# Tying the later weight splits of two out-projection rows behind a hidden-block sum on VectorE

## The chip, the cores and the metric

The kernel runs on one core of a Trainium2 chip. The metric is the device time in microseconds of one execution. Three executions of the kernel before took 1464.35, 1462.27 and 1464.3 us, with a median of 1464.3 us. Five engines with their own instruction queues do the work: TensorE (PE, with its weight loads shown as PEld), VectorE (DVE), ScalarE (ACT), GpSimd (POOL) and SyncE (SP, which issues most of the transfers here). Each engine takes its instructions in the order in which the program lists them.

## The reference

The reference is one inference step of a two-layer streaming encoder. Layer 0 is a convolution module, layer 1 is an attention over a shared key and value projection, and each is followed by a SwiGLU feed-forward network (FFN). The model width is 1024, the hidden width of the FFN is 2816, and there are 640 frames (512 of one new stream and 8 x 16 of running streams), all in float32. The change lies in the FFN, which is called twice:

```python
def swiglu_ffn(h, g, w_in, w_out):
    a, b = jnp.split(rms_norm(h, g) @ w_in, 2, axis=-1)
    return h + (jax.nn.silu(a) * b) @ w_out
```

The outputs are the normed trunk of both groups, the convolution buffers, and the shared key and value rows.

## The kernel before, in words

**Products of three matmuls.** Each float32 factor is split in two parts: a rounded high part, which ScalarE writes (L369), and the rest as a low part, which VectorE makes by a subtraction (L370). This is the function `put`; for a piece of a weight it is called through `cut`. A product of two split factors takes three matmuls in L436: high weight by high data, low weight by high data, high weight by low data. One such matmul has 128 x 128 weights and 320 data columns.

**Blocks of the FFN.** The 640 columns are held as two halves of 320, and both matrices of a product are cut in 2 x 2 blocks. Seven block products take the place of eight, after Strassen. The operands of the seven are named X11, X21, XT2, XT1, XT3, XT4 and X22; the ones with T are sums of blocks. The hidden rows are worked on in three chunks of six tiles (`NCH` = 3, `CW` = 6), and a rest behind them. In a chunk, `seven` does the in-projection of a tile; the two tiles of a pair give the blocks of which `combined` makes the seven hidden operands. When the second block of a pair is ready, the branch `else` of `sink` makes the gate product (L474), the sum for XT2 (`minus`, L474), its parts (`own(XT2, t1)`), the sum for XT3 (L513) and that for XT4 (L474), each with its high part on ScalarE and its low part on VectorE. The trace calls these operands `hid` and the sums they are cut from `B`.

**The out-projection.** `out_chunk` multiplies the chunk's seven hidden operands with four weight rows, u = 0 to 3. The order of the products is written out in the string `QORD`; a token such as `61` means product 6 of row 1, where 5 is XT1, 1 is X11, 2 is X21, 6 is XT2, 3 is X22, 7 is XT3 and 4 is XT4. A mark ' stands for the first two of three hidden tile pairs, and " for the third one alone:

```python
QORD = ("50' a0 a1 10' 50\" 10\" 20 60' 30' 51' 60\" 30\" 51\" 70 "
        "11 21 40 61 31 52 71 12 22 41 62 32 53 72 13 23 42 63 33")
```

So 60", 30" and 51" are short (three, three and three matmuls) and 70 follows them. `a0` and `a1` are the end of the last in-projection tile, which gives the second block of the last pair. Every product is followed by an addition of its PSUM bank to the trunk `h` on VectorE (L573). Products 1, 6, 7 and 4 of a row accumulate in one bank, so that 60" can only go on once the addition after 10" has read it, and 70 once that after 60" has; 62 waits in the same way for the addition after 12.

**The weight row.** `w_seven(..., True)` loads a row of four pieces by SP (L412, tile `raw`, 768 KB), makes the sum `s` of two pieces by two transfers that GpSimd issues (L415, L416), and cuts the seven weight operands in the order XT1, X11, X21, XT2, X22, XT3, XT4. Three sums on VectorE stand between the cuts: L420 and L421 before the cut of XT2, L423 before that of X22. There are two `raw` buffers, so the transfer of row u = 3 waits until the pieces of row u = 1 have been read for the last time, and the transfer for the next in-projection tile (1024 KB) waits for row u = 2. The split operands go into eleven slots (`whi`/`wlo` and `shi`/`slo`), which are used in turn.

**What sets the order.** The instructions are not executed in the order in which the code is written. A planner simulates the program and places each instruction on its engine; work inside `tc.high_priority(offset=HP)` goes ahead of other work. `behind(ins)` (and `tc.issue_after`) adds an edge for the planner: an instruction inside it is placed behind `ins` if it runs on the same engine as `ins`. No semaphore is added by it, and instructions of other engines are not bound. `put_end[0]` holds the last low part that VectorE was given, and `lead` a list of ties that the next cuts take one by one.

Of the kernel before, what the change touches and what calls it, by code (L numbers as in the profile page):

```python
# [15 lines left out]
P = 128  # L16
# [45 lines left out]
X11, X21, XT2, XT1, XT3, XT4, X22 = range(7)  # L62
# [20 lines left out]
def tile_trunk(ctx, tc, xT, vecs, hist, w_pw1, w_pw2, w_in0, w_out0, w_os0, w_in1, w_out1, w_os1,  # L83
# [52 lines left out]
    @contextmanager  # L136
    def behind(*ins):
        with ExitStack() as st:
            for i in ins:
                st.enter_context(tc.issue_after(i))  # L140
            yield
# [189 lines left out]
    def ffn(l, w_in, w_out, w_os, tail, hf, lead=(), b0=None):  # L331
# [16 lines left out]
        mm = fpool("mm2", 6, space=PSUM)  # L348
        tp = fpool("tp1", 2)
        wx = fpool("wx", 2)  # L350
        lead, put_end = list(lead), [None, None]

        def ties():
            return lead.pop(0) if lead else ()
# [17 lines left out]
        def cut(w, o, src):  # L372
            c = slice(o, o + src.shape[-1])
            put(w[0][:, c], w[1][:, c], src)
# [30 lines left out]
                            cut(*ws[j // 512], raw[:, j:j + n])  # L405
            return ws[1], ws[0], ws[2], ws[3]

        def w_seven(src, out=False):
            n = src.shape[-1] // 4
            raw, ws = wraw(), {}  # L410
            s1 = wx.tile([P, 512], F32, tag="s1", name=nm("s1"))[:, :n]
            nc.sync.dma_start(raw[:, :4 * n], src)  # L412
            a12, a11, a21, a22 = (raw[:, n * i:n * i + n] for i in range(4))
            with tc.high_priority(offset=HP), behind(*ties()):
                nc.gpsimd.dma_start(s1, src[:, 2 * n:3 * n])  # L415
                nc.gpsimd.dma_start(s1, src[:, 3 * n:4 * n], accum_op=add)  # L416
                for x in ((XT1, X11, X21, XT2, X22, XT3, XT4) if out else
                          (X11, X21, XT2, XT1, XT3, XT4, X22)):
                    if x == XT2:
                        nc.vector.tensor_tensor(out=a21, in0=a11, in1=a21, op=add)  # L420
                        nc.vector.tensor_tensor(out=a11, in0=s1, in1=a11, op=add)  # L421
                    elif x == X22:
                        nc.vector.tensor_tensor(out=a12, in0=a12, in1=a11, op=add)  # L423
                    ws[x] = slot()
                    cut(*ws[x], {XT1: s1, X11: a11, X21: a12, XT2: a11, X22: a12, XT3: a21,
                                 XT4: a22}[x])
            return ws

        def product(pt, w, xs, first, ks=None):
# [53 lines left out]
        def combined(HH, HL, kp, second, held, neg, early=None):  # L483
            def own(c, src):
                for H_, j in ((HH, 2 * HIX[c]), (HL, 2 * HIX[c] + 1)):
                    if kp == 0:
                        t = two(j)
                        H_[c] = [t[:, 0, :], t[:, 1, :]]
                    elif kp == 2:
                        H_[c].append(one(j))  # L490
                put(HH[c][kp], HL[c][kp], src)

            def sink(half, a, b):
                if early is not None and half == 0:
                    t = early
                else:
                    tag = f"B{half}{int(second)}"
                    t = tp.tile([P, NH], F32, tag=tag, name=nm(tag), bufs=1)
                with tc.high_priority(offset=HP):
                    gate(t, a, b, neg)  # L500
                    if half == 0:
                        own((X11, X21)[second], t)
                        held[second] = t
                    elif not second:
                        nc.vector.tensor_tensor(out=held[0], in0=held[0], in1=t, op=sub)
                        own(XT1, held[0])
                        held[2] = t
                    else:
                        t1, b21, b12 = held
                        minus(t1, t1, t)  # L510
                        own(XT2, t1)
                        own(X22, t)
                        nc.vector.tensor_tensor(out=b12, in0=t, in1=b12, op=sub)  # L513
                        own(XT3, b12)
                        minus(b21, t1, b21)
                        own(XT4, b21)
            return sink
# [32 lines left out]
        def out_chunk(c, HH, HL, after):  # L550
            ws, pts = {}, {}
# [5 lines left out]
            def go(i, u, part):  # L557
                if u not in ws:
                    o = (4 * c + u) * 12 * P
                    ws[u] = w_seven(w_os[:, o:o + 12 * P], True)  # L560
                b, x, first, half, row = prod[i]
                if first and part != '"':
                    pts[b, u] = mmt()[:, :NH]
                pt = pts[b, u]
                with tc.issue_after(last[0]) if last else nullcontext():
                    ins = product(pt, ws[u][x], list(zip(HH[x], HL[x])), first,
                                  {"": None, "'": (0, 1), '"': (2,)}[part])
                last[:] = [ins.ins]
                if part == "'":
                    return  # L570
                hv = h[:, 2 * u + row, half * NH:half * NH + NH]
                with tc.high_priority(offset=HP):
                    nc.vector.tensor_tensor(out=hv, in0=hv, in1=pt, op=sub if row else add)  # L573
# [1083 lines left out]
```

## Time and profile before

| what | value |
|---|---|
| median of three executions | 1464.3 us |
| time of the profiled execution | 1464.42 us |
| span of the profiled execution | 1462.5 us |
| mean granted TensorE clock | 0.998 |
| TensorE matmul busy | 1435.3 us, 98% of the span |
| TensorE weight load busy | 1371.7 us, 94% |
| VectorE busy | 1141.8 us, 78% |
| ScalarE busy | 756.4 us, 52% |
| GpSimd busy | 294.4 us, 20% |

The span is what lies between the first and the last instruction in the trace; 1.9 us of the execution's own time lie around it. Rows of the timeline give the start in us, the duration in us, the engine, the line, the operation, the tiles written and read, and in brackets how long the engine was idle before it and what released it. Matmuls overlap, so the duration of one (0.31 us) is more than the distance from one to the next (0.147 us where TensorE waits for nothing).

### The profile page before, as it was taken

To read this page: it belongs to the slowest core of one execution; us is meant where nothing else is said; L and a number is where in the kernel's file an instruction comes from. 1 tells how busy PE (TensorE), PEld (TensorE's weight loads), DVE (VectorE), ACT (ScalarE), POOL (GpSimd) and SP (SyncE) were. 2 spreads that over 40 slices of the span, in tenths; PEclk is the share of its full clock that TensorE was granted. 3 is DMA by queue.
4 is the path that set the end of the run, shared out by engine and by line. 5 is a ranking of instruction groups with operands and counts; after the bars stand their busy time and mean duration, and the time that the engine had idled before them with its cause. 6 is when DMAs were issued, how large, how long until landed. Compare 5 with 4: busy or idle time off the path is not lost.

```text
span 1462.5 us, 28255 instructions
## 1 busy us (share of the span) xinstructions
PE 1435.3 (98%) x11040; PEld 1371.7 (94%) x11040; DVE 1141.8 (78%) x2524; ACT 756.4 (52%) x1627; POOL 294.4 (20%) x349
## 2 busy tenths in 40 slices
PE   9999999999999999999999999999999999999998
PEld 8998799999999999999987898878999999999998
DVE  6789767899788789766768668576899888888755
ACT  4666544554554464445655455443565554455443
POOL 5699102011111111013222111011001111111101
PEclk9999999999999999999999999999999999999999
DMA  7267425045444445424655554461235444444522
GB/s 243 82 176 186 121 73 159 9 128 153 127 105 131 131 116 143 116 87 171 203 163 199 175 199 163 134 206 41 69 81 142 132 116 132 133 120 114 151 65 72
DMA packets 66932, 192.56 MB, mean 132 GB/s; under 512 B 12144, under 2 KB 30320, under 8 KB 58480
## 3 DMA queue, kind: packets, MB, share of 16 engines
q1 hardware_dynamic: 52432, 160.58, 33.9%
q0 software_dynamic: 13504, 29.37, 9.9%
q8 instruction: 86, 1.41, 0.4%
q10 hardware_dynamic: 864, 0.83, 0.2%
q14 instruction: 46, 0.38, 0.1%
HBM read 179.14 MB, written 11.61 MB: 130 GB/s over the span
## 4 chain that ended last, share of the span: by engine, by line
PE 75%; DVE 11%; POOL 4%; DMA 4%; issue 3%; ACT 3%; SPq 0%; DVEq 0%; POOLq 0%; ACTq 0%
PE mm L436 45%; PE mm L199 7%; PE mm L201 7%; PE mm L200 7%; POOL ca L830 3%; DVE w L820 2%; PE am L1307 1%; DMA raw<-in_w_in 1%; PE w L1323 1%; PE am L1354 1%; DVE wlo L370 1%; PE am L1290 1%; DVE hid L591 1%; PE w L1266 1%; PE mm L874 1%
## 5 line engine op out<-in xcount | busy, mean ns | idle before, releaser
L436 PE MATMUL mm<-XH,whi 128*128 128x320 f32 x896 | 275.8, 310 | 1.7 <-DVE t L451 0.7
L436 PE MATMUL mm<-XH,wlo 128*128 128x320 f32 x896 | 276.7, 309 | 0.0
L436 PE MATMUL mm<-XL,whi 128*128 128x320 f32 x896 | 274.7, 309 | 0.0
L369 ACT ACTIVATE whi<-raw 128x512 fp32r<-128x512 f32 (+2 forms) x280 | 169.2, 614 | 142.6 <-PE mm L436 114.3
L199 PE MATMUL mm<-xh,whi 128*128 128x320 f32 (+2 forms) x640 | 200.9, 315 | 1.2 <-ACT xh L187 0.8
L370 DVE TENSOR_TENSOR wlo<-raw,whi 128x512 fp32r<-128x512 f32 (+2 forms) x280 | 184.2, 666 | 21.4 <-ACT whi L369 20.2
L200 PE MATMUL mm<-xh,wlo 128*128 128x320 f32 (+2 forms) x640 | 198.9, 312 | 0.0
L201 PE MATMUL mm<-xl,whi 128*128 128x320 f32 (+2 forms) x640 | 197.1, 312 | 0.4 <-DVE xl L189 0.4
L436 PE MATMUL mm<-hid,whi 128*128 128x320 f32 x732 | 171.9, 310 | 2.4 <-DVE hid L370 2.2
L436 PEld LDWEIGHTS mm<-XH,whi 128*128 128x128 f32 x896 | 167.7, 188 | 3.4 <-ACT t L446 1.7
L436 PEld LDWEIGHTS mm<-XH,wlo 128*128 128x128 f32 x896 | 168.3, 188 | 0.0
L436 PEld LDWEIGHTS mm<-XL,whi 128*128 128x128 f32 x896 | 167.7, 188 | 0.0
L436 PEld LDWEIGHTS mm<-hid,whi 128*128 128x128 f32 x732 | 124.8, 188 | 4.7 <-DVE hid L370 3.2
L199 PEld LDWEIGHTS mm<-xh,whi 128*128 128x128 f32 x640 | 121.0, 189 | 4.4 <-ACT xh L187 2.0
L201 PEld LDWEIGHTS mm<-xl,whi 128*128 128x128 f32 x640 | 120.4, 189 | 1.3 <-DVE xl L189 0.8
L200 PEld LDWEIGHTS mm<-xh,wlo 128*128 128x128 f32 x640 | 121.1, 189 | 0.2
L436 PE MATMUL mm<-hid,wlo 128*128 128x320 f32 x366 | 113.0, 309 | 0.0
L436 PE MATMUL mm<-XL,shi 128*128 128x320 f32 x344 | 105.8, 309 | 2.1 <-DVE XL L370 2.1
L436 PE MATMUL mm<-XH,shi 128*128 128x320 f32 x344 | 106.1, 309 | 0.0
L436 PE MATMUL mm<-XH,slo 128*128 128x320 f32 x344 | 106.0, 308 | 0.0
L415 POOL DMA_DIRECT2D s<-in_w_in x38 | 22.0, 579 | 382.3 <-DVE wlo L370 205.5
L830 POOL TENSOR_TENSOR ca<-ca,cvt 128x512 f32<-128x512 f32 x60 | 91.9, 1532 | 17.7 <-ACT cvt L827 11.2
(272 smaller groups left out, 3367.0 us busy)
## 6 DMA issues: line engine op xcount, KB each, us to landing
raw<-in_w_in SPq DMA_DIRECT2D x38, 1024.0 KB
s<-in_w_in POOLq DMA_DIRECT2D x76, 256.0 KB, 4.2
raw<-in_w_os SPq DMA_DIRECT2D x24, 768.0 KB
cache<-in_ck SPq DMA_DIRECT2D x32, 512.0 KB
cache<-in_cv SPq DMA_DIRECT2D x32, 512.0 KB
raw<-in_w_pw SPq DMA_DIRECT2D x11, 1024.0 KB
s<-in_w_os POOLq DMA_DIRECT2D x48, 192.0 KB, 3.7
raw<-in_w_kq SPq DMA_DIRECT2D x8, 1024.0 KB
```

What stands on the lines that cost most here:

```text
L199: nc.tensor.matmul(ps, wh, xh, start=(first and i == 0), stop=False)
L200: nc.tensor.matmul(ps, wl, xh, start=False, stop=False)
L201: end = nc.tensor.matmul(ps, wh, xl, start=False, stop=(stop and i == last))
L369: put_end[1] = nc.scalar.activation(out=hi, in_=src, func=AF.Copy).ins
L370: put_end[0] = nc.vector.tensor_tensor(out=lo, in0=src, in1=hi.bitcast(F32), op=sub).ins
L415: nc.gpsimd.dma_start(s1, src[:, 2 * n:3 * n])
L436: last = nc.tensor.matmul(pt, wt, v, start=(first and k == i == 0), stop=(k == n - 1 and i == 2), skip_group_check=True)
L591: nc.vector.scalar_tensor_tensor(out=t[k], in0=h[:, k0 + k, half * NH:half * NH + NH], scalar=col(V_NFFN + l * KT, k0 + k), in1=bcw[half], ...
L820: tap_end[0] = nc.vector.scalar_tensor_tensor(out=dst, in0=src, scalar=wj, in1=dst, op0=ALU.mult, op1=ALU.add).ins
L830: nc.gpsimd.tensor_tensor(out=acc, in0=acc, in1=pr, op=ALU.add)
L874: conv_end[0] = nc.tensor.matmul(pt[32 * q:32 * q + 32, 0:n], w4[0:r, 4 * tg + q, :], mv, start=(tg == 0), stop=(tg == 7)).ins
L1266: nc.tensor.matmul(ps, QQ[:, q], KK[:, 0:n], start=True, stop=False)
```

## The change

The low part of XT2 of the second block is remembered in `xt2_end`. It is written anew for each pair of tiles, so that at the out-projection it holds that of the chunk's last pair. For weight row u = 1 the cuts of X22, XT3 and XT4 are placed behind it; for row u = 2 the whole row is put behind it through `lead`. Since the remembered instruction runs on VectorE, the edge binds VectorE's instructions of these cuts: the low parts L370, and for row u = 2 the sums L420, L421 and L423 too. No instruction is added and none removed.

```diff
@@ -348,7 +348,7 @@
-        lead, put_end = list(lead), [None, None]
+        lead, put_end, xt2_end = list(lead), [None, None], [None]
@@ -405,7 +405,7 @@
-        def w_seven(src, out=False):
+        def w_seven(src, out=False, tie=()):
@@ -422,8 +422,9 @@
                     ws[x] = slot()
-                    cut(*ws[x], {XT1: s1, X11: a11, X21: a12, XT2: a11, X22: a12, XT3: a21,
-                                 XT4: a22}[x])
+                    src = {XT1: s1, X11: a11, X21: a12, XT2: a11, X22: a12, XT3: a21, XT4: a22}[x]
+                    with behind(*(tie if x in (X22, XT3, XT4) else ())):
+                        cut(*ws[x], src)
@@ -509,6 +510,7 @@
                         own(XT2, t1)
+                        xt2_end[0] = put_end[0]
                         own(X22, t)
@@ -557,7 +559,9 @@
                     o = (4 * c + u) * 12 * P
-                    ws[u] = w_seven(w_os[:, o:o + 12 * P], True)
+                    if u == 2:
+                        lead.append((xt2_end[0],))
+                    ws[u] = w_seven(w_os[:, o:o + 12 * P], True, (xt2_end[0],) if u == 1 else ())
```

The line numbers of VectorE's rows shift: L474 becomes L475, L513 becomes L515 and L573 becomes L577. The instructions of SP and GpSimd keep their order. On ScalarE two pairs of neighbours swap; on TensorE some matmuls shift by a place or so later in the chunks, and at the start of the second FFN three matmuls move ahead of those of the norm's statistics.

The first place is on VectorE in chunk 0 of the first FFN, where the second block of the last pair is made. `raw_3910` is weight row u = 1 and `raw_4013` row u = 2; `hid_3855` is the low part of XT2, `hid_3859`, `hid_3864` and `hid_3869` those of X22, XT3 and XT4. `mm_3872` is the bank of products 10, 60 and 70, `mm_3887` that of 20. The row just ahead of these twelve in the order before is the sum L420 of `raw_4013`.

```order
L370 TENSOR_TENSOR slo_2846<-raw_3910,shi_2845 128x384
L370 TENSOR_TENSOR wlo_2844<-raw_3910,whi_2843 128x384
L573 TENSOR_TENSOR h<-h,mm_3887 128x320
L370 TENSOR_TENSOR slo_2848<-raw_3910,shi_2847 128x384
L474 SCALAR_TENSOR_TENSOR B_421_3707<-B_421_3707,B_436_3851 128x320
L513 TENSOR_TENSOR B_424_3741<-B_436_3851,B_424_3741 128x320
L370 TENSOR_TENSOR hid_3859<-B_436_3851,hid_3858 128x320
L474 SCALAR_TENSOR_TENSOR B_433_3831<-B_421_3707,B_433_3831 128x320
L370 TENSOR_TENSOR hid_3855<-B_421_3707,hid_3854 128x320
L370 TENSOR_TENSOR hid_3864<-B_424_3741,hid_3863 128x320
L370 TENSOR_TENSOR hid_3869<-B_433_3831,hid_3868 128x320
L573 TENSOR_TENSOR h<-h,mm_3872 128x320
```

In the changed kernel the same stretch of VectorE's order, which begins with the addition for `mm_3887` (here left out), goes on as follows.

```order
L475 SCALAR_TENSOR_TENSOR B_421_3707<-B_421_3707,B_436_3851 128x320
L515 TENSOR_TENSOR B_424_3741<-B_436_3851,B_424_3741 128x320
L370 TENSOR_TENSOR hid_3859<-B_436_3851,hid_3858 128x320
L475 SCALAR_TENSOR_TENSOR B_433_3831<-B_421_3707,B_433_3831 128x320
L370 TENSOR_TENSOR hid_3855<-B_421_3707,hid_3854 128x320
L370 TENSOR_TENSOR wlo_2844<-raw_3910,whi_2843 128x384
L370 TENSOR_TENSOR slo_2846<-raw_3910,shi_2845 128x384
L370 TENSOR_TENSOR slo_2848<-raw_3910,shi_2847 128x384
L420 TENSOR_TENSOR raw_4013<-raw_4013 128x384
L370 TENSOR_TENSOR hid_3864<-B_424_3741,hid_3863 128x320
L370 TENSOR_TENSOR hid_3869<-B_433_3831,hid_3868 128x320
L577 TENSOR_TENSOR h<-h,mm_3872 128x320
```

The three low parts of row u = 1 and the sum of row u = 2 moved from ahead of the low part of XT2 to the places right behind it. The addition for `mm_3872` still closes the group, with the same instructions ahead of it.

The second place is on VectorE a few microseconds later in the same chunk, at the fourth weight row (`raw_4108`, u = 3) and the next in-projection tile (`raw_4203`). `mm_4056` is the bank of products 12 and 62, and the rows of before are these.

```order
L573 TENSOR_TENSOR h<-h,mm_3961 128x320
L370 TENSOR_TENSOR slo_2846<-raw_4108,shi_2845 128x384
L423 TENSOR_TENSOR raw_4108<-raw_4108 128x384
L573 TENSOR_TENSOR h<-h,mm_4056 128x320
L420 TENSOR_TENSOR raw_4203<-raw_4203 128x512
L370 TENSOR_TENSOR wlo_2842<-raw_4108,whi_2841 128x384
```

In the changed kernel the rows at this place read as follows.

```order
L577 TENSOR_TENSOR h<-h,mm_3961 128x320
L370 TENSOR_TENSOR slo_2846<-raw_4108,shi_2845 128x384
L420 TENSOR_TENSOR raw_4203<-raw_4203 128x512
L423 TENSOR_TENSOR raw_4108<-raw_4108 128x384
L577 TENSOR_TENSOR h<-h,mm_4056 128x320
L370 TENSOR_TENSOR wlo_2842<-raw_4108,whi_2841 128x384
```

The sum L420 of the next in-projection tile, which needs that tile's transfer, now stands ahead of L423 and of the addition for `mm_4056`.

The third place is on VectorE in chunk 1 of the first FFN, where `raw_5116` is row u = 1, `raw_5219` row u = 2, `hid_5061` the low part of XT2, `mm_5018` the bank of products 50 and 30, `mm_5078` that of 10, 60 and 70. The twelve rows of before are these, with the sum L420 of `raw_5219` three rows ahead of them.

```order
L370 TENSOR_TENSOR hid_5040<-B_541_5037,hid_5039 128x320
L451 TENSOR_TENSOR t_535_4966<-mm_4968,t_535_4966 128x320
L370 TENSOR_TENSOR slo_2850<-raw_5116,shi_2849 128x384
L573 TENSOR_TENSOR h<-h,mm_5018 128x320
L573 TENSOR_TENSOR h<-h,mm_5078 128x320
L474 SCALAR_TENSOR_TENSOR B_544_5057<-t_535_4966,t_537_4993 128x320
L370 TENSOR_TENSOR wlo_2842<-raw_5116,whi_2841 128x384 x2
L474 SCALAR_TENSOR_TENSOR B_529_4913<-B_529_4913,B_544_5057 128x320
L513 TENSOR_TENSOR B_532_4947<-B_544_5057,B_532_4947 128x320
L573 TENSOR_TENSOR h<-h,mm_5093 128x320
L370 TENSOR_TENSOR hid_5065<-B_544_5057,hid_5064 128x320
L370 TENSOR_TENSOR wlo_2842<-raw_5116,whi_2841 128x384
```

In the changed kernel the stretch behind the addition for `mm_5018` reads as follows.

```order
L577 TENSOR_TENSOR h<-h,mm_5018 128x320
L475 SCALAR_TENSOR_TENSOR B_544_5057<-t_535_4966,t_537_4993 128x320
L577 TENSOR_TENSOR h<-h,mm_5078 128x320
L475 SCALAR_TENSOR_TENSOR B_529_4913<-B_529_4913,B_544_5057 128x320
L515 TENSOR_TENSOR B_532_4947<-B_544_5057,B_532_4947 128x320
L370 TENSOR_TENSOR hid_5065<-B_544_5057,hid_5064 128x320
L577 TENSOR_TENSOR h<-h,mm_5093 128x320
L475 SCALAR_TENSOR_TENSOR B_541_5037<-B_529_4913,B_541_5037 128x320
L370 TENSOR_TENSOR hid_5061<-B_529_4913,hid_5060 128x320
L370 TENSOR_TENSOR wlo_2842<-raw_5116,whi_2841 128x384 x3
L420 TENSOR_TENSOR raw_5219<-raw_5219 128x384
```

Three low parts of row u = 1 and the sum of row u = 2 moved behind the low part of XT2 here too. VectorE's order changes in the same way in chunk 2 and in the three chunks of the second FFN.

## The prediction

> **What bounds the kernel now.** I read the busy shares first, then the chain that ended last, then the waits of TensorE's weight loads, and then, for the places that the change touches, the timelines of TensorE and VectorE. The busy shares and the chain's shares are these:
>
> ```profile
> PE 1435.3 (98%) x11040; PEld 1371.7 (94%) x11040; DVE 1141.8 (78%) x2524; ACT 756.4 (52%) x1627; POOL 294.4 (20%) x349
> PE 75%; DVE 11%; POOL 4%; DMA 4%; issue 3%; ACT 3%; SPq 0%; DVEq 0%; POOLq 0%; ACTq 0%
> ```
>
> TensorE is busy for 98% of the 1462.5 us span. The change adds and removes no instruction, so it can only move TensorE's waits. Those that it can reach stand in the waits of the weight loads (us in total, times, longest one):
>
> ```profile
> PEld mm L436 <- DVE hid L370: 4.8, 6, 0.8
> PEld mm L436 <- ACT hid L369: 1.7, 2, 0.8
> PEld mm L436 <- DVE h L573: 1.0, 6, 0.2
> ```
>
> There are six out-projection chunks, three in each FFN. TensorE waits six times for a low part of a hidden sum, twice for a high part, and six times for an addition to the trunk. The first two rows together are 6.5 us, 0.44% of the time: that is all that an earlier XT2 could free. The rows of chunk 0 of the first FFN show where they lie.
>
> ```profile
> 331.55 0.31 PE L436 MATMUL mm<-hid,shi 128*128 128x320 f32 x1
> ...
> 335.08 0.19 PEld L436 LDWEIGHTS mm<-hid,shi 128*128 128x128 f32 x1 [0.84 <-ACT hid L369]
> 336.18 0.19 PEld L436 LDWEIGHTS mm<-hid,shi 128*128 128x128 f32 x1 [0.81 <-DVE hid L370]
> ...
> 337.38 0.19 PEld L436 LDWEIGHTS mm<-hid,whi 128*128 128x128 f32 x1 [0.17 <-DVE h L573]
> ```
>
> The last matmul of product 20 starts at 331.55. Product 60" waits twice, for XT2's high part and for its low part, 1.65 us together. Then 30" and 51" run, and 70 waits once more, at 337.38, for the addition after 60". VectorE over the same time:
>
> ```profile
> 331.37 0.48 DVE L474 SCALAR_TENSOR_TENSOR B<-t,t 128x320 f32<-128x320 f32 x1
> 331.77 0.55 DVE L420 TENSOR_TENSOR raw<-raw 128x384 f32<-128x384 f32 x1
> 332.24 0.55 DVE L370 TENSOR_TENSOR slo<-raw,shi 128x384 fp32r<-128x384 f32 x1
> 332.71 0.55 DVE L370 TENSOR_TENSOR wlo<-raw,whi 128x384 fp32r<-128x384 f32 x1
> 333.18 0.47 DVE L573 TENSOR_TENSOR h<-h,mm 128x320 f32<-128x320 f32 x1
> 333.57 0.54 DVE L370 TENSOR_TENSOR slo<-raw,shi 128x384 fp32r<-128x384 f32 x1
> 334.04 0.48 DVE L474 SCALAR_TENSOR_TENSOR B<-B,B 128x320 f32<-128x320 f32 x1
> 334.44 0.48 DVE L513 TENSOR_TENSOR B<-B,B 128x320 f32<-128x320 f32 x1
> 334.85 0.48 DVE L370 TENSOR_TENSOR hid<-B,hid 128x320 fp32r<-128x320 f32 x1
> 335.25 0.48 DVE L474 SCALAR_TENSOR_TENSOR B<-B,B 128x320 f32<-128x320 f32 x1
> 335.65 1.28 DVE L370 TENSOR_TENSOR hid<-B,hid 128x320 fp32r<-128x320 f32 x3
> 336.86 0.47 DVE L573 TENSOR_TENSOR h<-h,mm 128x320 f32<-128x320 f32 x1
> ```
>
> No row has a wait in brackets, and each start follows the last by 0.40 us (320 columns) or 0.47 us (384 columns). VectorE is saturated from the gate product at 331.37 to the addition at 336.86, which ends at 337.33; TensorE's 70 follows at 337.38. So it is the sum of VectorE's work up to that addition that sets when 70 starts, and not the order within it.
>
> **The change part by part.** *The splits behind XT2.* In chunk 0 three low parts and one L420, 4 x 0.47 = 1.88 us, go from ahead of XT2 to behind its low part. That part then ends near 334.38 (gate to 331.77, the addition of product 20 to 332.30, then B, b12, one low part, B and XT2's low part at 0.40 each plus the 0.48 of the last), and 60", which is free to start at 335.08 - 0.84 = 334.24, wants it two matmuls of 0.15 us later, near 334.5. Both of its waits go, since the high part, made behind B from 332.8 on, is there sooner still. But the same rows of VectorE still stand ahead of the addition after 60", so 70 can't start earlier than before. The 1.65 us turn up as a longer wait at 70, and the gain is 0.
>
> *The addition pulled forward.* Behind the gate the changed order has the addition after 20, which reads a bank whose last matmul starts at 331.55. How long an addition must stay behind its last matmul I take from chunk 1:
>
> ```profile
> 442.45 0.31 PE L436 MATMUL mm<-hid,whi 128*128 128x320 f32 x1
> ...
> 442.33 0.55 DVE L370 TENSOR_TENSOR slo<-raw,shi 128x384 fp32r<-128x384 f32 x1
> 442.80 0.93 DVE L573 TENSOR_TENSOR h<-h,mm 128x320 f32<-128x320 f32 x2
> ...
> 449.20 0.19 PEld L436 LDWEIGHTS mm<-hid,whi 128*128 128x128 f32 x1 [0.17 <-DVE h L573]
> ```
>
> That is 442.80 - 442.45 = 0.35 us. In chunk 0 the addition then starts at 331.90 instead of the free place at 331.77, and everything behind it, 70 too, is 0.12 us late. In chunk 1 the L420 that stood ahead of these rows goes, so the place of this addition (product 50) comes 0.47 us earlier, at about 442.39, while TensorE still ends when it does: VectorE idles 0.41 us, and 70 starts at 449.61 instead of 449.20. I take 0.41 for the four chunks that begin so (1 and 2 of both FFNs).
>
> Of this, a part comes back at product 62, which waits for the addition after 12:
>
> ```profile
> 462.38 0.69 DVE L420 TENSOR_TENSOR raw<-raw 128x512 f32<-128x512 f32 x1 [1.14 <-DMA raw<-in_w_in]
> 463.00 0.55 DVE L423 TENSOR_TENSOR raw<-raw 128x384 f32<-128x384 f32 x1
> 463.46 0.48 DVE L573 TENSOR_TENSOR h<-h,mm 128x320 f32<-128x320 f32 x1
> ...
> 464.06 0.19 PEld L436 LDWEIGHTS mm<-hid,whi 128*128 128x128 f32 x1 [0.33 <-issue]
> ```
>
> VectorE stood 1.14 us for the transfer of the next in-projection tile, the addition ended at 463.94, and TensorE followed at 464.06 after 0.33 us of idleness. If that transfer lands when it did, a TensorE that comes 0.41 us later waits 0.33 us less: net 0.08 us a chunk, 4 x 0.08 = 0.3 us. The ends are 0 and 4 x 0.41 = 1.6 us.
>
> *The fourth row's transfer.* SP issues it once the pieces of row 1 have been read, and the last of them is one of the moved splits:
>
> ```profile
> 334.14 0.33 SPq L412 DMA_DIRECT2D raw<-in_w_os  x1
> 339.13 0.56 DVE L420 TENSOR_TENSOR raw<-raw 128x384 f32<-128x384 f32 x1 [0.54 <-DMA raw<-in_w_os]
> ...
> 349.39 0.56 DVE L423 TENSOR_TENSOR raw<-raw 128x384 f32<-128x384 f32 x1
> 349.87 0.48 DVE L573 TENSOR_TENSOR h<-h,mm 128x320 f32<-128x320 f32 x1
> 350.58 0.69 DVE L420 TENSOR_TENSOR raw<-raw 128x512 f32<-128x512 f32 x1 [0.24 <-DMA raw<-in_w_in]
> 352.00 0.31 PE L436 MATMUL mm<-hid,whi 128*128 128x320 f32 x1
> ```
>
> In chunk 0 that split ended at 334.11 and SP issued at 334.14; in the changed order it ends at 335.79, 1.68 us later. The transfer took 339.13 - 334.14 = 4.99 us and VectorE already waited 0.54 us for it, so its L420 now starts near 340.8. VectorE catches up while TensorE works on products 70 to 21, so I cost that stall at nothing; if the catch-up fails, it costs up to 1.68 us here.
>
> Nearer is what follows. The next tile's L420, which must wait for a transfer landing near 350.56, now stands ahead of L423 and of the addition after 12. Before, that addition started at 349.87 and 62 at 352.00 without a wait. In the changed order the addition comes 0.62 + 0.47 us after the L420's start, so 351.67 to 352.15, and 62 starts 0.19 us late if the transfer lands as before, 0 if it lands half a microsecond earlier, 0.5 if 0.3 later. I take 0.25 for the first FFN. In the second the L420 did not wait:
>
> ```profile
> 1130.84 0.48 DVE L573 TENSOR_TENSOR h<-h,mm 128x320 f32<-128x320 f32 x1
> 1131.24 0.68 DVE L420 TENSOR_TENSOR raw<-raw 128x512 f32<-128x512 f32 x1
> ...
> 1132.97 0.31 PE L436 MATMUL mm<-hid,whi 128*128 128x320 f32 x1
> ```
>
> Here 62 starts at 1132.97, 2.1 us after the addition's start, and the transposition of 1.1 us is covered: 0.
>
> By the Trainium skill's page "DMA: Bandwidth & Descriptors", section "Anatomy of one DMA — SWDGE (gpsimd) path", a transfer costs about 2.0 us plus its bytes at 436 GB/s, on that path; for 768 KB my estimate from it is 3.8 us. The trace shows 4.99 us on SP's queue, so I stay with the trace. By the page's figure the fourth row would land 1.2 us earlier, the stall would go, and my sum would be about 0.25 us lower.
>
> *What else moves.* The start of the second FFN, where three matmuls move ahead of the norm's statistics, and ScalarE's two swaps I cost at nothing, with TensorE's other work as cover; if that is gone, three matmuls at 0.15 us, 0.4 us, either way.
>
> *The sum.* 2 x 0.12 + 0.3 + 0.25 = 0.8 us. Against the profiled execution's own 1464.42 us that is 1465.2 us. This execution stands 0.12 us above the median of the three runs, far less than the 2.1 us between them.
>
> **The rivals.** *The waits at 60" are really gained (faster).* This is so if the addition after 60" does not hold 70: the full 6.5 us would go, 1457.9 us. Half of it, 1461 us, would come if the planner's order let VectorE reach the addition without the moved splits. For it speaks that 60" waits longest of all; against it, the third row of waits: 70 already waits in all six chunks for that addition.
>
> *The late fourth row holds TensorE (slower).* If VectorE can't catch up, its queue, which takes work in order, passes the delay on to the additions, and TensorE waits for banks. The price is the delay of the transfer: 1.68 us in the two chunks 0, and in chunks 1 and 2, where the last split now stands behind two more rows of 0.40 us and the 0.41 us of idleness and has one of 0.47 us less ahead of it, 0.74 us: 2 x 1.68 + 4 x 0.74 = 6.3 us, 1470.7 us. It decides from where the fourth row's L420 starts so late that the addition after 12 starts behind about 351.5 in chunk 0. For it speaks that VectorE waits for both transfers already (0.54, 0.24, 1.14); against it, that those waits came back before TensorE felt more than 0.33 us.
>
> *The clock falls in a longer wait (slower).* The waits at 60" and 70 become one of about 1.65 + 0.17 + 0.12 = 1.9 us in chunk 0. The trace has one dip to look at (PE, PEld, DVE, ACT, POOL busy, clock):
>
> ```profile
> 180.00:185.00 5.00, 5.00 (x43) 5.00 (x41) 1.79 (x4) 3.43 (x8) 0.00 (x0) 1.00 0.00 0
> 185.00:190.00 5.00, 5.00 (x28) 5.00 (x27) 1.34 (x4) 0.46 (x1) 0.00 (x0) 0.66 0.00 0
> ```
>
> A mean clock of 0.66 over 5 us costs 5 x 0.34 = 1.7 us; six of them would give 10.2 us, 1475 us. Against it: two waits of 0.8 us close together in each chunk 0 leave the clock of the run at 0.998 today. The page "TensorE: Matmul & The Clock Gate" of the Trainium skill, Part 1, puts the fall at an idle window of about 3.4 us; by that rule these waits are too short, and no run here shows the length.
>
> *The change does nothing.* The tie is an edge for the planner alone. But VectorE's rows did move, so this only means the same time by another way, within the forecast.
>
> **How the numbers follow.** My forecast (wait moves from 60" to 70, some tenths lost) gets 0.58, with 1463.5 to 1467.3 as its own range: from the ends above, 0.24 us to 0.24 + 1.6 + 0.5 + 0.4 = 2.7 us, and the spread of the runs on the low side. The gained waits get 0.14, the late fourth row 0.24, the clock 0.04. The predicted time is 1465.2 us. The range leaves out the clock, half of the gained waits and a quarter of the late row, and goes from 1461.0 to 1469.8 us. About 0.2%, 2.9 us, is what a measurement of this kernel can tell from no change. Faster by more than that: 0.14. Slower by more: of the late row and the clock nearly all, and a small part of the forecast's upper end, 0.29. Within: 0.57.
>
> **What would show it.** Right: in the changed trace the rows of 60" lose their waits for `hid`, and the row of waits for the additions to `h` grows from 1.0 us to about 9 us over six waits (1.9 in each chunk 0; in the other four 0.8 + 0.17 + 0.41 = 1.4, where 0.8 is the fourth part of 6.5 - 2 x 1.65); the fourth row's L420 in chunk 0 starts near 340.8 after a wait of about 0.8 us; 70 starts within half a microsecond of its old place in each chunk. Wrong: 70's wait stays at 0.2 us while 60" has lost its own (the gain is real), or a new wait of a microsecond stands at 62 or 13 (the fourth row), or the clock row of a slice falls below 0.9.

## The result, and the profile after

The changed kernel takes 1470.44 us in the median of six executions (1469.22 to 1471.42), the kernel before beside it 1463.2 us (1461.79 to 1464.35). The ratio is 1.0049 with a 95% interval of 1.0038 to 1.0059: the change makes the kernel slower by 7.2 us, where 1465.2 us was forecast and the range ended at 1469.8.

The profiled execution of the changed kernel took 1469.32 us with a span of 1467.2 us, only 4.7 us longer than that of before. Part of the rest is a matter of the two executions shown. The dip of TensorE's clock between 185 and 190 us, which the prediction quotes, is not in the profiled execution of the changed kernel (clock 1.00 in that window), so that TensorE reaches the first out-projection about 1 us earlier by the clock than it did before.

The waits of TensorE's weight loads in the changed kernel (us in total, times, longest one), of the products of the FFN:

```profile
PEld mm L437 <- DVE h L577: 9.6, 6, 2.0
PEld mm L437 <- issue: 5.7, 6, 2.3
```

The two rows for `hid` are gone. ("issue" is idle time that the profile puts down to no other instruction; the row of the matmul itself, below, names the addition.) The wait for the addition to `h` has grown from 1.0 to 9.6 us, and a group put down to "issue" from 1.4 us over four waits to 5.7 us over six. The two rows are 15.3 us; the four that answer to them in the kernel before (4.8, 1.7 and 1.0, quoted in the prediction, and the 1.4 here) were 8.9.

```profile
PEld mm L436 <- issue: 1.4, 4, 0.4
```

That is 6.4 us more, against 7.2 us in the medians. The first of the two rows is the wait of product 70. In chunk 0 of the first FFN it reads so, on VectorE and then on TensorE's weight loads:

```profile
330.28 0.48 DVE L475 SCALAR_TENSOR_TENSOR B<-t,t 128x320 f32<-128x320 f32 x1
330.81 0.49 DVE L577 TENSOR_TENSOR h<-h,mm 128x320 f32<-128x320 f32 x1
...
332.83 0.48 DVE L370 TENSOR_TENSOR hid<-B,hid 128x320 fp32r<-128x320 f32 x1
333.23 0.55 DVE L370 TENSOR_TENSOR wlo<-raw,whi 128x384 fp32r<-128x384 f32 x1
333.70 1.02 DVE L370 TENSOR_TENSOR slo<-raw,shi 128x384 fp32r<-128x384 f32 x2
334.64 0.55 DVE L420 TENSOR_TENSOR raw<-raw 128x384 f32<-128x384 f32 x1
335.11 0.89 DVE L370 TENSOR_TENSOR hid<-B,hid 128x320 fp32r<-128x320 f32 x2
335.91 0.48 DVE L577 TENSOR_TENSOR h<-h,mm 128x320 f32<-128x320 f32 x1
...
336.44 0.19 PEld L437 LDWEIGHTS mm<-hid,whi 128*128 128x128 f32 x1 [1.97 <-DVE h L577]
```

XT2's low part is ready at 333.31, and 60" runs without a wait. The splits follow, and the addition after 60" ends at 336.39: the two waits of 0.84 and 0.81 us have become one of 1.97.

The other row is product 62. The chain of waits through it, and VectorE and TensorE there:

```profile
343.55 8.01 DMA raw<-in_w_in
351.56 0.02 issue
351.58 0.69 DVE raw L420
352.28 0.47 DVE raw L423
352.75 0.41 DVE h L577
353.15 0.14 issue
353.29 0.83 PE mm L437 x4
```

```profile
351.58 0.69 DVE L420 TENSOR_TENSOR raw<-raw 128x512 f32<-128x512 f32 x1 [3.16 <-DMA raw<-in_w_in]
352.19 0.55 DVE L423 TENSOR_TENSOR raw<-raw 128x384 f32<-128x384 f32 x1
352.66 0.48 DVE L577 TENSOR_TENSOR h<-h,mm 128x320 f32<-128x320 f32 x1
...
353.29 0.39 PE L437 MATMUL mm<-hid,whi 128*128 128x320 f32 x1 [2.07 <-DVE h L577]
```

VectorE stands idle for 3.16 us with the L420 of the next in-projection tile at the head of its queue. The transfer for it took 8.01 us; before it was 5.5. The addition after 12, behind the L420, is late, and 62 waits 2.07 us for it. By the starts of TensorE's matmuls, the distance at 62 is 2.23 us longer than 0.147 us in this chunk and 0.46, 1.09, 0.48, 0.43 and 0.56 us longer in the other five, 5.3 us in all; the row of 5.7 us counts the idle time of the weight loads at the same six places.

### The profile page after: what moved, and what is told of

Read it like the earlier page. It is cut to its first block, busy times and chain, and to the rows that moved or that the text cites. A ratio compares the mean times of both kernels' runs of the same rounds, so it can differ in the third digit from the quotient of the medians.

```text
span 1467.2 us, 28248 instructions
## 1 busy us (share of the span) xinstructions
PE 1434.4 (98%) x11040; PEld 1372.5 (94%) x11040; DVE 1140.4 (78%) x2524; ACT 757.4 (52%) x1627; POOL 296.0 (20%) x349
## 3 DMA queue, kind: packets, MB, share of 16 engines
q8 instruction: 86, 1.41, 0.4%
## 4 chain that ended last, share of the span: by engine, by line
PE 83%; DVE 7%; DMA 5%; ACT 2%; issue 1%; POOL 1%; DVEq 0%; ACTq 0%; POOLq 0%
PE mm L437 44%; PE mm L199 10%; PE mm L201 9%; PE mm L200 9%; DMA raw<-in_w_in 4%; PE mm L878 2%; DMA raw<-in_w_os 1%; PE am L1311 1%; PE w L1327 1%; DVE wlo L370 1%; PE am L1294 1%; ACT whi L164 1%; PE am L1358 1%; DVE h L577 1%; PE mm L146 1%
## 5 line engine op out<-in xcount | busy, mean ns | idle before, releaser
L370 DVE TENSOR_TENSOR wlo<-raw,whi 128x512 fp32r<-128x512 f32 (+2 forms) x280 | 183.8, 666 | 21.4 <-ACT whi L369 19.4
```

Of the source, the lines that this page charges most:

```text
L370: put_end[0] = nc.vector.tensor_tensor(out=lo, in0=src, in1=hi.bitcast(F32), op=sub).ins
```

## The experiments

The open points were these. Is it the order of VectorE's queue that makes 62 wait (theory A), or is VectorE late by itself, because the fourth row of weights comes later (theory B)? Why does the next tile's transfer take longer? And what would it take to gain what 60" waited for?

### The next tile behind the addition after 12

The edit ties VectorE's work on the next in-projection tile behind the addition after product 12, in the changed kernel and, as `next_back_b`, in the kernel before.

```diff
             def go(i, u, part):
...
-                    nc.vector.tensor_tensor(out=hv, in0=hv, in1=pt, op=sub if row else add)
+                    ha = nc.vector.tensor_tensor(out=hv, in0=hv, in1=pt, op=sub if row else add).ins
+                if (i, u) == (1, 2):
+                    add12[0] = ha
...
+            lead.append((add12[0],))
             return lambda i: go((7, 4)[i], 3, "")
```

> The changed kernel, with VectorE's work on the next in-projection tile tied behind the addition after product 12, so that its L420 again stands behind L423 and that addition. Theory A (the order of VectorE's queue: an L420 that waits for a transfer stands ahead of the addition that frees the bank of 62): TensorE's waits at 62, 5.3 us over six chunks in the changed kernel, fall below 1 us; the waits at 70 stay at about 9.6 us; the time falls from 1470.4 to about 1465.5 us, ratio to the kernel before 1.001 to 1.002. Theory B (VectorE is late by itself, because the fourth row comes later): the waits at 62 stay at 4 us or more and the ratio at 1.004 to 1.005.

> The kernel before with the same tie of the next in-projection tile behind the addition after 12; its order changes in chunks 1 and 2 of both FFNs alone, where the L420 stood ahead of that addition already. Theory A: the waits at 62 of 0.15 to 0.37 us in these four chunks, 1.06 us together, go; ratio 0.9993. Theory B: they stay; ratio 1.000.

With it the changed kernel takes 1464.41 us beside 1463.62 for the kernel before, ratio 1.0006 (0.9998 to 1.0015). The kernel before with the same tie takes 1462.43 us, ratio 0.9992 (0.998 to 1.0004). The waits of the first, and VectorE at the place where the changed kernel lost 2 us:

```profile
PEld mm L437 <- DVE h L577: 9.8, 7, 2.0
```

```profile
350.51 0.48 DVE L577 TENSOR_TENSOR h<-h,mm 128x320 f32<-128x320 f32 x1
352.90 0.69 DVE L420 TENSOR_TENSOR raw<-raw 128x512 f32<-128x512 f32 x1 [1.91 <-DMA raw<-in_w_in]
```

The "issue" row is gone. VectorE still waits 1.91 us for the transfer, but behind the addition, where TensorE does not feel it. Theory A holds: six of the seven microseconds lost were the order of L420 and the addition. The 0.8 us that stay are close to the 0.9 us by which the rows together are longer than before (9.8 against 4.8 + 1.7 + 1.0 + 1.4 = 8.9): 2.1 us more at 60" and 70, 0.2 us at one product behind 62, and 1.4 us less at 62. In the kernel before, where the same order stands in chunks 1 and 2, the "issue" row goes too, and the median falls by 1.2 us, though the interval does not exclude no change.

### One tie at a time

```diff
-                    if u == 2:
-                        lead.append((xt2_end[0],))
                     ws[u] = w_seven(w_os[:, o:o + 12 * P], True, (xt2_end[0],) if u == 1 else ())
```

This is `u1_only`; `u2_only` keeps the two lines and leaves the last argument empty.

> Only the tie of row u = 1 (X22, XT3 and XT4 behind XT2's low part); row u = 2 is not tied. Its L420 stays ahead of the gate's followers as in the kernel before, so no addition is pulled forward and 70 starts when it did: the waits at 60" and 70 together stay at 7.2 us. The fourth row's transfer comes as late as in the changed kernel, and in chunk 0 the next tile's L420 stands ahead of the addition after 12. Theory A: waits at 62 of 3 to 5 us, time 1466 to 1468 us, ratio 1.002 to 1.003. If the extra at 70 were what costs: ratio 1.000.

> Only the tie of row u = 2; the splits of row u = 1 stay ahead of XT2. The fourth row's transfer is issued about as in the kernel before, but the next tile's L420 stands ahead of the addition after 12 in chunk 0 too, and the addition after 50 is pulled forward in chunks 1 and 2 (0.41 us at 70 in each). Theory A: waits at 62 of 1.5 to 3 us, ratio 1.002. Theory B: without a late fourth row the waits at 62 are those of the kernel before, 1 us, and the ratio is 1.001.

The tie of row 1 alone takes 1472.1 us beside 1463.62, ratio 1.0058 (1.0045 to 1.0071), worse than expected and worse than both ties. That of row 2 alone takes 1465.25 us, ratio 1.0012 (1.0003 to 1.002). Their waits, row 1 alone first:

```profile
PEld mm L437 <- issue: 9.4, 6, 2.9
PEld mm L437 <- DVE h L575: 7.6, 6, 1.6
PEld mm L437 <- DVE hid L370: 0.5, 2, 0.3
```

```profile
PEld mm L437 <- DVE hid L370: 4.7, 6, 0.8
PEld mm L437 <- DVE h L577: 3.9, 6, 0.6
PEld mm L437 <- ACT hid L369: 0.7, 2, 0.4
PEld mm L437 <- issue: 0.7, 1, 0.7
```

With row 1 alone tied, 60" and 70 wait 8.1 us where they waited 7.5, so the net there is nearly nothing, while 62 waits 9.4 us, where 3 to 5 were expected. With row 2 alone tied, the L420 of the next tile stands ahead of the addition after 12 as well, and yet 62 waits once only, for 0.7 us; I had expected 1.5 to 3 by theory A. So the order is what lets a late transfer through to TensorE, but that the transfer is late comes from the tie of row 1. Theory A was right on the one half and said nothing on the other.

### Why the transfer is late

SP issues the next tile's transfer when row 2 has been read. With row 2 alone tied that took 5.5 us in chunk 0, from SP's issue to VectorE's start:

```profile
347.07 0.33 SPq L412 DMA_DIRECT2D raw<-in_w_in  x1
...
352.58 0.69 DVE L420 TENSOR_TENSOR raw<-raw 128x512 f32<-128x512 f32 x1 [1.56 <-DMA raw<-in_w_in]
```

In the changed kernel GpSimd's second transfer into the sum `s` of the same tile (L416, the one that adds to what the first has put there) is issued just ahead of SP's; in the kernel before it came just behind. The rows are GpSimd and SP of before, then the same of the changed kernel, in chunk 0:

```profile
345.05 0.33 SPq L412 DMA_DIRECT2D raw<-in_w_in  x1
...
345.83 0.86 POOL L416 DMA_DIRECT2D s<-in_w_in  x1 [3.09 <-DMA s<-in_w_in]
```

```profile
342.92 0.86 POOL L416 DMA_DIRECT2D s<-in_w_in  x1 [3.08 <-DVE h L577]
...
343.55 0.33 SPq L412 DMA_DIRECT2D raw<-in_w_in  x1
```

So SP comes 0.78 us ahead of GpSimd before and 0.63 us behind it in the changed kernel. (The buffer of `s` comes free at L421 of row 2, which in the changed order stands ahead of the L420 of the fourth row instead of behind it: GpSimd's first transfer into `s` follows the end of that L421 by 0.7 us in both kernels, at 342.17 us before and at 339.26 us in the changed one.) Theory C was that the transfer takes longer for that reason. The first try took another tile for `s`:

```diff
+            wx.tile([P, 512], F32, tag="s1", name=nm("s1"))
             return lambda i: go((7, 4)[i], 3, "")
```

> The changed kernel, the same instructions in the same order on every engine; alone the tile of the next in-projection tile's sum s takes the other of its two buffers, so that GpSimd's two transfers into it wait until row u = 3 has read its own. Theory C (the next tile's transfer takes 6.1 to 8.0 us instead of 5.1 to 5.5 because GpSimd's second transfer is queued ahead of it): the next tile's raw transfer takes 5.0 to 5.6 us again, TensorE's waits at 62 fall from 5.3 us to 1 to 2.5 us, time about 1467 us, ratio 1.002 to 1.003. Without that cause: the transfer still takes more than 6 us and the ratio stays at 1.005.

It changed nothing: GpSimd's second transfer was issued at 342.80 us, 0.70 us ahead of SP's (0.63 without the edit): the tile that nobody writes held nothing back. The time of 1470.04 us (ratio 1.0044, 1.003 to 1.0058) only repeats the changed kernel, and as a trial of theory C the run decides nothing. The second try puts a copy of one column on GpSimd ahead of the two transfers, which reads what L421 of the fourth row wrote:

```diff
+                if a11_3 is not None and not out:
+                    nc.gpsimd.tensor_copy(out=s1[:, 0:1], in_=a11_3[:, 0:1])
                 nc.gpsimd.dma_start(s1, src[:, 2 * n:3 * n])
                 nc.gpsimd.dma_start(s1, src[:, 3 * n:4 * n], accum_op=add)
```

> The changed kernel with a copy of one column on GpSimd ahead of the next in-projection tile's two sum transfers; the copy reads what L421 of row u = 3 wrote, so these transfers can't start before that, some 3 us after the raw transfer is issued. VectorE's order up to product 62 is that of the changed kernel (the L420 stands ahead of the addition after 12). Theory C (the raw transfer takes longer because GpSimd's accumulating transfer is queued ahead of it): it takes 5.0 to 5.6 us in all six chunks, where the changed kernel has 6.1 to 8.0, and the waits at 62 fall from 5.3 to 1 to 3 us. Without that cause: 6 us and more, waits at 62 of 4 us or more. The sum s comes later, which may cost TensorE something in the next in-projection tile; the total is not what this run is read for.

```profile
344.45 0.33 SPq L415 DMA_DIRECT2D raw<-in_w_in  x1
...
347.79 0.18 POOL L419 COPY s<-raw 128x1 f32<-128x1 f32 x1 [15.84 <-DVE raw L426]
348.44 1.14 POOL L420 DMA_DIRECT2D s<-in_w_in  x2 [0.47 <-issue]
```

```profile
349.32 0.69 DVE L425 TENSOR_TENSOR raw<-raw 128x512 f32<-128x512 f32 x1 [0.19 <-DMA raw<-in_w_in]
```

The row of two transfers at 348.44 holds the first one of this tile and the first one of the next; the adding one (here L421) follows only at 352.08, 7.6 us behind SP's issue. The transfer now takes 349.32 - 344.45 = 4.9 us to VectorE's start, and between 4.75 and 4.96 us to its landing in all six chunks; the changed kernel's six are 8.01, 6.19, 6.72, 6.20, 6.13 and 6.25. None of the waits at 62 is left, although the L420 (L425 in this run) stands ahead of the addition. So GpSimd's transfers are what makes this one late.

The edit moves both of them and by a long way, so alone it does not show that the place of the second decides. The twelve traces of this document (six chunks each; some of the kernels follow below) fall into three groups by that place:

| GpSimd's adding transfer is issued | traces | the 1024 KB take, from SP's issue to the landing |
|---|---|---|
| 6.4 us or more behind SP's | the two with the copy | 4.69 to 4.99 us |
| from 0.25 us ahead to 0.78 us behind | before, the same with the next tile behind addition 12, row 2 alone | 5.14 to 5.74 us |
| 0.54 to 1.97 us ahead | the other seven | 5.94 to 8.01 us |

The groups do not overlap, so theory C holds for the transfer with one correction: being first is not the limit, since four transfers of the kernel with row 2 alone tied, with the adding one 0.14 to 0.25 us ahead, took 5.2 to 5.4 us. In the last two groups the first transfer into `s` moves with the second (2.9 to 3.8 us ahead in the one, 4.2 us or more in the other), and these traces can't tell the two apart. Why the last group reaches from 5.94 to 8.01 us stays open. The sum itself comes so late, however, that the kernel takes 1497.78 us (ratio 1.0236, 1.0216 to 1.0257). VectorE's L421 (here L426) waits 6.99 us for it at the head of the queue, and additions stand behind:

```profile
362.08 0.69 DVE L426 TENSOR_TENSOR raw<-s,raw 128x512 f32<-128x512 f32 x1 [6.99 <-DMA s<-in_w_in]
...
365.43 0.19 PEld L442 LDWEIGHTS mm<-hid,whi 128*128 128x128 f32 x1 [4.09 <-DVE h L582]
```

It is the same fault as at 62, made larger: an instruction that waits for a transfer ahead of an addition that TensorE waits for.

### The splits behind the addition after 60"

What 60" waited for was not gained, since the splits still stood ahead of the addition on which 70 waits. In this kernel the cuts of X22, XT3 and XT4 of row 1 are written out behind that addition and tied behind it, and so is row 2.

```diff
-                    with behind(*(tie if x in (X22, XT3, XT4) else ())):
-                        cut(*ws[x], src)
+                    if late is not None and x in (X22, XT3, XT4):
+                        late.append((ws[x], src))
+                    else:
+                        cut(*ws[x], src)
...
+                    ha = nc.vector.tensor_tensor(out=hv, in0=hv, in1=pt, op=sub if row else add).ins
+                    if (i, u) == (6, 0):
+                        add60[0] = ha
+                        with behind(ha):
+                            for ww, src in late:
+                                cut(*ww, src)
...
                     if u == 2:
-                        lead.append((xt2_end[0],))
+                        lead.append((add60[0],))
```

> The changed kernel with its ties moved on: the cuts of X22, XT3 and XT4 of row u = 1 are written out behind the addition after 60" and tied behind that addition, as is the whole of row u = 2, so that the addition on which 70 waits stands ahead of the three splits and of the L420. In this order the next tile's L420 stands behind the addition after 12 in all six chunks. Theory A (70 waits because the splits stand ahead of its addition in VectorE's queue, 62 because the L420 does): 60" and 70 together wait less than 1.5 us where the kernel before waits 7.2 us, 62 less than 1 us; time about 1456.5 us, ratio 0.995. Rival (VectorE has too much work in this stretch, in any order; the wait only moves on once more, to 61, 31 or 62): the sum of waits in the chunks stays at 7 us or more and the ratio at 1.000.

> The kernel with the splits behind the addition after 60" once more, beside the one above on the same chip: ratio 0.994 to 0.997 as measured first (0.9959).

Measured first, it took 1457.9 us beside 1464.28, ratio 0.9959 (0.9944 to 0.9974); measured once more, 1458.14 us beside 1463.21, ratio 0.9958 (0.9945 to 0.997). This kernel is faster than both others, by 6.4 and 5.1 us than the one before. VectorE around the addition, and the waits left:

```profile
333.73 1.29 DVE L370 TENSOR_TENSOR hid<-B,hid 128x320 fp32r<-128x320 f32 x3
334.93 0.48 DVE L579 TENSOR_TENSOR h<-h,mm 128x320 f32<-128x320 f32 x1
335.33 0.55 DVE L370 TENSOR_TENSOR wlo<-raw,whi 128x384 fp32r<-128x384 f32 x1
335.80 1.02 DVE L370 TENSOR_TENSOR slo<-raw,shi 128x384 fp32r<-128x384 f32 x2
336.74 0.55 DVE L420 TENSOR_TENSOR raw<-raw 128x384 f32<-128x384 f32 x1
```

```profile
PEld mm L439 <- DVE h L579: 2.5, 5, 0.6
```

No wait at 60", 70 or 62 is left; the 2.5 us lie behind 62, at 72, which waits for the addition after 62, and the L420 of the next tile stands ahead of that one. So the rival was right to a part: one wait did move on. In the second profile the row is 4.1 us over six. Two kernels try to take these too: `late62` ties the next tile behind the addition after 62; `late_s` adds the copy on GpSimd.

> The kernel with the splits behind the addition after 60" (ratio 0.996), with the next in-projection tile tied behind the addition after 62 as well, so that its L420 stands behind the addition for which that kernel's remaining waits (2.5 us, five of up to 0.6 us) are. Theory A (queue order alone): these waits go, ratio 0.994 to 0.995. Rival (VectorE's later start of the next tile is paid in the next in-projection): ratio 0.996 to 0.998, with new waits outside the out-projection.

> The kernel with the splits behind the addition after 60" and the same copy on GpSimd. Theory C: the next tile's raw transfer falls from 6.5 to 6.9 us to 5.0 to 5.6 us here too, and the five waits at or behind 62 of 0.24 to 0.54 us go; ratio to the kernel before 0.994 to 0.996, if the late sum costs nothing. Otherwise the ratio is 0.996 or more.

The one takes 1458.18 us (ratio 0.9967, 0.9955 to 0.9978), the other 1461.23 us (ratio 0.9984, 0.9975 to 0.9994). In `late62` the waits behind 62 are gone, but those for `t` in the in-projection, 1.7 us over four waits without it, are now these:

```profile
PEld mm L439 <- ACT t L449: 4.8, 8, 0.8
```

What was saved in the one place is lost in the other, as the rival said. In `late_s` the transfer takes 4.69 to 4.99 us and the waits behind 62 are gone, as theory C had it, but the time is outside its 0.994 to 0.996: the same row for `t` reads 5.0 us, and two new waits of 0.93 and 0.97 us stand where a later tile's L420 waits for its transfer ahead of an addition.

### The sum of the waits beside the times

If the account is right, the sum of the rows at 60", 70 and 62 should give the time of each kernel. All sums are less the 8.9 us of the kernel before, and all times less the median of the kernel before that was measured beside it:

| kernel | rows at 60", 70, 62 (us) | less 8.9 | time less before |
|---|---|---|---|
| changed | 9.6 + 5.7 | +6.4 | +7.2 |
| the changed one with the unused tile | 9.6 + 5.7 | +6.4 | +5.8 |
| next tile behind addition 12 | 9.8 | +0.9 | +0.8 |
| the same in the kernel before | 4.8 + 1.7 + 1.0 | -1.4 | -1.2 |
| tie of row 1 alone | 9.4 + 7.6 + 0.5 | +8.6 | +8.5 |
| tie of row 2 alone | 4.7 + 3.9 + 0.7 + 0.7 | +1.1 | +1.6 |
| splits behind addition 60" | 2.5 | -6.4 | -6.4 |
| the same, measured once more | 4.1 | -4.8 | -5.1 |

The rows follow the times within 0.8 us. The other three kernels have new waits in the in-projection, which count too: `late62` 3.1 us for `t`, so -8.9 + 3.1 = -5.8 against -5.0 measured; `late_s` 1.9 + 3.3 + 0.4, so -3.3 against -2.1; the changed kernel with the copy is taken up in the last section. The row for a kernel is that of one execution, the time a median.

## Why the prediction was wrong

**The wait moves from 60" to 70.** This was right, in size too. About 9 us over six waits were forecast for that row, and 9.6 were measured; XT2's low part came before 60" wanted it. The addition pulled forward costs 0.41 us in chunks 1 and 2: the distance to the matmul before at 70 is 1.30 us too long in each of these four chunks, with the next one 0.11 behind it, 1.41 together, as forecast.

**Product 62.** Here the step failed. It was summed as -0.33 us in four chunks (it "comes back") and +0.25 us in one, and rested on the clause "if that transfer lands when it did". The transfer did not. In chunk 1 it was given to VectorE at 462.38 before and at 464.38 after, 2.0 us later, while TensorE was 1.8 us later there (at product 70) than in the kernel before:

```profile
456.84 0.33 SPq L412 DMA_DIRECT2D raw<-in_w_in  x1
```

```profile
458.17 0.33 SPq L412 DMA_DIRECT2D raw<-in_w_in  x1
...
464.38 0.69 DVE L420 TENSOR_TENSOR raw<-raw 128x512 f32<-128x512 f32 x1 [1.34 <-DMA raw<-in_w_in]
```

SP's issue came 1.3 us later (the upper row is of before), with TensorE, and the transfer took 6.2 us instead of 5.5. So nothing came back. In chunk 0 the L420 started at 351.58 on a TensorE that ran about 1 us ahead, where a landing between 350.1 and 350.9 was assumed, and 62 lost 2.2 us instead of 0.25. In chunk 0 of the second FFN, where the cost was put at 0, the weight loads waited 0.55 us. Over six chunks the waits at 62 rose from 1.4 to 5.7 us, +4.3, where the sum had -1.3 + 0.25. That term alone is 5.3 us off, and the rows together are 5.6 us above the sum of 0.8. Two chunks of the first FFN make up 3.2 of the 4.3 us: chunk 0, where the transfer took 8.01 us, and chunk 2, where it took 6.72. The order that let this through was in the prediction, and the price of it was taken from a landing time that the change itself moved, both with the issue and with the length of the transfer. Its end of the range, 0.5 us, was set by no more than 0.3 us of scatter of that time.

**The fourth row.** The L420 of the fourth row was to start near 340.8 us after a wait of 0.8. It started at 338.96, about 340 with the 1 us by which this execution ran ahead, without a wait to speak of. SP issued that transfer at 334.78, which with the same 1 us is the 335.8 of the forecast, but the 4.99 us that it took before are the longest of six: the other five of the kernel before, as far as VectorE waited for them, took 4.2 to 4.3 us, and so did the changed kernel's (4.18 us here), nearer to the 3.8 us that the prediction set aside. And the order of VectorE has L421 of row 2 and others ahead of that L420 now. That L421 in its turn freed GpSimd's buffer earlier, which the prediction did not follow: it looked at where POOL's transfers stand in the order, which is unchanged, and not at when their buffer comes free.

**The rival "late fourth row".** It gave 1470.7 us, and 1470.44 was measured, but that is luck: the time came through another door. The price was worked out as the delay of the fourth row, while the loss is at the next tile's transfer. Its condition was half right: VectorE's queue does pass a transfer's delay on to TensorE, from the point where the addition after 12 starts behind 351.5 (it started at 352.66).

**The rivals on the faster side and on the clock.** "Really gained" needed the addition after 60" not to hold 70. The kernel with the splits behind it shows what that is worth, 6.4 us and 5.1 us in two measurements, near what the rival priced (6.5), but it takes another order than that of this change. The nearness is in part luck: the 7.5 us at 60" and 70 and the 1.4 us at 62 all went, and 2.5 us (in the second profile 4.1) came behind 62. The clock did not fall: between 335 and 340 us, behind the wait of 1.97 us, it reads 1.00.

```profile
335.00:340.00 5.00, 3.56 (x24) 3.56 (x25) 5.00 (x13) 1.05 (x2) 0.58 (x1) 1.00 0.50 157
```

**The range.** Its upper end of 1469.8 us left out a quarter of the rival's case, and the time fell 0.6 us beyond it.

## What to carry to other kernels

To move work behind the operation that an engine waits for gains nothing if the next wait is for an instruction that still stands behind the same work; the place for it is behind the last of the instructions that are waited for, here the addition after 60", and that order was worth 5 to 6 us. In an engine's queue, look for an instruction that waits for a transfer and stands ahead of one on which a busier engine waits, and price it by the transfer's landing after the change: ask what frees the buffers of all transfers around it, and in which order they then reach the queues.

## What the runs showed of the hardware

A transfer of 1024 KB on SP's queue took 4.75 to 4.96 us with GpSimd's two transfers of 256 KB issued 4 us and more behind it (the six of the run with the copy), 5.1 to 5.5 us with the second of these issued 0.1 to 0.8 us behind it (the kernel before), and 6.1 to 8.0 us with it issued 0.6 to 0.9 us ahead (the changed kernel). I had taken its duration as fixed within 0.3 us.

The granted clock stayed at 1.00 behind TensorE's waits of 1.97 us, and behind the longest one of the kernel with row 1 alone tied, 2.92 us, too. It fell behind five of the six waits of 3.23 to 4.58 us in the run with the copy on GpSimd. The rows give the window, its length, the busy time of PE, PEld, DVE, ACT and POOL, then the granted clock. The first two are behind the waits of 4.09 us that ended at 365.43 and of 4.43 us that ended at 1278.52; the last two begin at the ends of two waits of 3.23 us, at 482.47 and at 599.41:

```profile
365.00:370.00 5.00, 4.57 (x20) 4.57 (x21) 5.00 (x10) 1.71 (x4) 0.00 (x0) 0.66 0.15 21
...
1278.00:1283.00 5.00, 4.48 (x17) 4.48 (x18) 5.00 (x11) 1.80 (x4) 0.00 (x0) 0.50 0.21 26
```

```profile
482.40:485.60 3.20, 3.13 (x12) 3.13 (x13) 3.20 (x8) 1.00 (x3) 0.00 (x0) 0.50 0.00 0
599.40:606.00 6.60, 6.58 (x45) 6.58 (x46) 6.60 (x13) 2.97 (x6) 0.57 (x1) 1.00 0.36 115
```

Two waits of the same length thus went different ways. The clock of that whole run is 0.989 against 0.998, by my estimate 0.009 x 1496 = 13 us. With the wait rows of 32.6 us (23.7 more than before) that makes some 37 us, of the size of the 34.5 us by which the run is slower; the estimate also counts the time at half clock in which TensorE stood idle. The Trainium skill's page "TensorE: Matmul & The Clock Gate", Part 1, puts the fall at an idle window of about 3.4 us and says that the clock is then half. The runs fit both: 0.50 in these windows, no fall behind waits of up to 2.92 us, one fall of two at 3.23 us, and a fall behind each of the waits of 3.48 us and more. The fall in the kernel before between 185 and 190 us, which the prediction quotes, is of another kind: TensorE is shown busy for all of the 5 us ahead of it, from 182.50 to 185.09 us with 24 matmuls of a single column each, and the same matmuls in the changed kernel's execution are followed by no fall. What decides there stays open.
